# A pooling mixer with its last 32 tokens on quarter-width column tiles, its norm folded into the pooling matrices, and h updated two tiles at a time

## The chip, the cores and the metric

The kernel runs on one core of one Trainium2 chip, in float32 and float32r. The metric is the device time of one launch in microseconds, the median over runs of the same program. Three runs of the kernel before took 953.94, 954.66 and 955.35 us, so its time is 954.66 us.

## The reference, cut to what matters

The program is a decoder trunk of two layers: 16 meta tokens and 256 input tokens (272 together), 1024 channels. Layer 0 mixes tokens with a causal pooling mixer, layer 1 with differential attention; each mixer stands between two SwiGLU feed-forward blocks, and each of these parts sits between two RMS norms. The change touches the pooling mixer of layer 0 alone:

```python
def causal_multiscale_pool(h, w, b, scale):
    ...
    for g, win in enumerate(POOL_WINDOWS):          # 2, 4, 8, 16
        lo = jnp.maximum(t + 1 - win, 0)
        cnt = (t + 1 - lo).astype(jnp.float32)
        pooled.append((csg[:, 1:, g] - csg[:, lo, g]) / cnt[None, :, None])
    pooled = jnp.stack(pooled, axis=2)
    diff = (pooled - hg).astype(h.dtype)
    y = jnp.einsum('blgc,gcd->blgd', diff, w) + b
    return y.reshape(bsz, L, D) * scale
...
    h = h + 0.5 * rmsnorm(f, ffn_norm_post[i, 0])
    hn = rmsnorm(h, mix_norm_pre[i])
    m = causal_multiscale_pool(hn, pool_w[j], pool_b[j], pool_scale[j])
    h = h + rmsnorm(m, mix_norm_post[i])
```

The 1024 channels fall into four groups of 256. Each group has its own window and its own 256x256 matrix `w`. The mean over a window and the subtraction of `hn` are linear in the tokens, so both together are a banded matrix over tokens.

## The kernel before, in words

Activations lie transposed: `h[j]`, j = 0 to 7, is a tile of 128 channels by 272 tokens, and `hall` is all eight side by side. Tokens are stored as the 256 inputs first and the 16 meta tokens last, although the meta tokens come first in time. Every engine works through a list of instructions in the order in which the code issues them (`manual_schedule`), and waits on semaphores that the tile framework puts in; an instruction that waits holds up all that stand behind it on its engine.

The mixer (`pool_mix`, L674 to L776) runs between the first feed-forward block and the second:

- **Residual.** The end of the first block has left its output in `btall`, a first value `old.y` of its post-norm (table lookup, L281) and its sum of squares. VectorE refines the norm by a Newton step (L505, L509) and adds the scaled block output to `h`: first tile 0 by itself (L701, L703, L704), then tile 1 and pairs of tiles (L708 product, L709 sum, sizes in `POOL_H`).
- **Inner product.** For each j, `inner(j)` (L687 to L691) multiplies `h[j]`, as the stationary operand, by `wps[j]`, 256 columns of the group's weights. There are three sets of tokens, `tok` (L680): 0 to 127, 128 to 255, and 144 to 271. The third exists for the 16 meta tokens and the first inputs' neighbours. Results are tokens by channels, in six PSUM banks `z[half][set]`, a half being two groups (512 channels). The two j of a group add up in the same columns.
- **Norm.** ScalarE squares `hall` pair by pair (L711), VectorE adds the squares up (L715 to L718), TensorE sums over the channels for each of the three token sets (L720), and `rsqrt` gives `r2`, one factor per token (L281, L275 to L277). Six of the eight `inner` steps stand ahead of these sums on TensorE and two behind them (`LATE = 2`).
- **Scaled copies.** `normed(q)` (L727 to L734) takes a half of z out of PSUM, multiplied by `r2`, into `zs`: ScalarE and VectorE three copies of 128x512 each.
- **Pooling.** `pooled(j)` (L736 to L751) multiplies `zs` by `bands`, the banded matrices, with three matmuls for each 128 output channels: the tokens 128 to 255, the tokens 0 to 143, and the 32 columns at both ends of y that depend on the meta tokens (L742, L743, L746). Then ScalarE squares the result for the post-norm (L453), and so on into the second feed-forward block, whose first matmuls are L522.

Three things set what waits for what. `warm` (L265) issues matmuls on a constant tile to keep TensorE at work where it would wait: `WARM0 = 12` ahead of the inner products and `WARM2 = 3` behind the pooling. `post.old(j)` (L424 to L431) is a ScalarE product of `h[j]` and a gain that the second feed-forward block needs, for the first three j (`AHEAD[1] = 3`); in the mixer it stands behind the squares (L723). Its output tile `a` is allocated with the tag `xlo{j}` (L426). The pooling weights `wps[q]` were allocated with the tag `xlo{q}` (L664). A tag has one buffer there, so `a` of j lies where `wps[j]` lay.

Line numbers are those of the kernel before. In the changed kernel the lines up to `pool_mix` are four lower: `post.old` is L426 there, the table lookup L277, `inner` L686.

Of the kernel before, what the change touches and what calls it, by code (L numbers as in the profile page):

```python
# [9 lines left out]
F32 = mybir.dt.float32  # L10
# [6 lines left out]
P = 128  # L17
D = 1024
# [34 lines left out]
LATE = 2  # L53

POOL_H = ((0, 1), (1, 2), (2, 4), (4, 6), (6, 8))
POOL_SQ = ((0, 2), (2, 4), (4, 6), (6, 8))
# [5 lines left out]
WARM0 = 12  # L62
# [117 lines left out]
def trunk(ctx, tc, ht, w13a, w13b, w2t, w2n, wqkva, wqkv, wo, wp, lamv, mask, band, gpost, out):  # L180
# [493 lines left out]
    def pool_mix(old, ps, post):  # L674

        def bank():
            return ps.tile([P, 512], F32, tag="bank", name="bank")


        tok = ((0, P), (P, 2 * P), (L - P, L))  # L680

        z = [[bank() for _ in tok] for _ in range(2)]
        sums = bank()[:, 0:3]
# [8 lines left out]

        with tc.tile_pool(name="poolw", bufs=1, reuse_waits="tile") as pw:
            sq = pw.tile([P, NK, L], F32, name="psq")
            zs = [pw.tile([P, D], F32, name=f"zs{ti}", tag=f"zs{ti}") for ti in range(3)]
# [4 lines left out]
            t = tmp.tile([P, L], F32, tag="rt", name="rt")  # L700
            nc.vector.tensor_tensor(t, btall[:, 0], old.y, ALU.mult)  # L701
            old.slope()
            nc.vector.scalar_tensor_tensor(t, old.c, 1.5, t, ALU.add, ALU.mult)  # L703
            nc.vector.tensor_tensor(h[0], h[0], t, ALU.add)  # L704
            old.finish()
            for lo, hi in POOL_H[1:]:
                t = pw.tile([P, 3, L], F32, tag="pt", name="pt", bufs=2)[:, :hi - lo]
                nc.vector.tensor_tensor(t, btall[:, lo:hi], old.r.unsqueeze(1).to_broadcast([P, hi - lo, L]), ALU.mult)  # L708
                nc.vector.tensor_tensor(hall[:, lo:hi], hall[:, lo:hi], t, ALU.add)  # L709
            for lo, hi in POOL_SQ:  # L710
                nc.scalar.activation(out=sq[:, lo:hi], in_=hall[:, lo:hi], func=AF.Square)  # L711
            for j in range(NK - LATE):
                inner(j)
            acc = pw.tile([P, 2, L], F32, name="pacc2")
# [12 lines left out]
            def normed(q):  # L727
                at = slice(q * 512, (q + 1) * 512)
                nc.scalar.mul(out=zs[0][:, at], in_=z[q][0], mul=r2[:, 0:1])
                nc.vector.tensor_scalar(zs[1][:, at], z[q][1], r2[:, 1:2], None, ALU.mult)  # L730
                if q:
                    nc.vector.tensor_scalar(zs[2][:, at], z[q][2], r2[:, 2:3], None, ALU.mult)
                else:
                    nc.scalar.mul(out=zs[2][:, at], in_=z[q][2], mul=r2[:, 2:3])  # L734

            def pooled(j):  # L736
# [5 lines left out]
                nc.tensor.matmul(y[:, P:SEQ], lhsT=zs[1][:, c], rhs=bands[:, g, 0:P], start=True, stop=True)  # L742
                nc.tensor.matmul(y[:, 0:P + NMETA], lhsT=zs[0][:, c], rhs=bands[:, g, 0:P + NMETA],  # L743
                                 start=False, stop=True, skip_group_check=True)
                ends = y.rearrange("p (a b) -> p a b", b=SEQ)[:, :, 0:NMETA]
                nc.tensor.matmul(ends, lhsT=zs[2][:, c],  # L746
                                 rhs=bands[:, g, P + NMETA:].rearrange("p (a b) -> p a b", b=NMETA),
                                 start=False, stop=True, skip_group_check=True)
                post.squared(j, y[:, :L], vt[:, C_PS + j:C_PS + j + 1], pbs[:, j:j + 1], add=False)
# [540 lines left out]
```

## Time and profile before

| what | value |
|---|---|
| median of three runs | 954.66 us (953.94 to 955.35) |
| the profiled execution, its own time | 954.47 us |
| span of that execution, first to last instruction | 952.7 us |
| TensorE matmul rows busy | 940.8 us (99%) |
| weight loads busy | 904.5 us (95%) |
| VectorE, ScalarE, GpSimd busy | 637.2, 501.9, 14.7 us |

The profile is of one execution on the chip. Its times run in microseconds from the span's start. A line of its timeline reads: start, length, engine, source line, operation, output<-inputs, shape, how many instructions were merged into the line, and in brackets how long the engine had stood idle before it and what ended that. PE is TensorE, DVE VectorE, ACT ScalarE, POOL GpSimd. A float32 matmul leaves two records, so 24 records are 12 matmuls. A line of a group reads: source line, engine, operation, names, shape, count, then busy time, mean nanoseconds of one, and idle time before. A line of the windows reads: from:to, length, then busy time and count of PE, PEld (weight loads), DVE, ACT and POOL, then the granted clock of TensorE (1.00 is full speed), the share of DMA and GB/s. The mixer lies between about 206 and 230 us.

### The profile page before, as it was taken

Reading aid. Unit: us, or ns where it says so; the run is one execution under the profiler, and the core shown is the slowest. Engines: PE = TensorE matmul, PEld = TensorE weight load, DVE = VectorE, ACT = ScalarE, POOL = GpSimd, SP = SyncE. Lnnn points to the kernel's source line nnn. Section 1 sums busy time; section 2 is a strip of 40 time slices with the busy share of each in tenths; the row PEclk is TensorE's granted clock in tenths of the full one; section 3 lists DMA queues with packets and bytes.
Section 4 is the critical chain, followed back from the end, with each engine's and each line's share of the span. In section 5 each row is a group of like instructions: output and inputs, shape, how many; then the busy total and the mean of one; then the engine's idle time right before and its main releaser. Section 6 shows DMA issues by size and latency. Waiting matters only on the chain.

```text
span 952.7 us, 17430 instructions
## 1 busy us (share of the span) xinstructions
PE 940.8 (99%) x6937; PEld 904.5 (95%) x6937; DVE 637.2 (67%) x1094; ACT 501.9 (53%) x863; POOL 14.7 (2%) x22
## 2 busy tenths in 40 slices
PE   9999999999999999999999999999999999999997
PEld 9999999998999999999999999999998998888885
DVE  7955554458975555448955554468876899767774
ACT  7744444435654445545744455446776756445442
POOL 0000000210000000000000000000001000000000
PEclk9999999999999999999999999999999999999999
DMA  9755557630375556551755556532523628655521
GB/s 337 239 204 177 166 155 222 219 119 2 116 267 174 175 159 192 179 195 42 257 194 177 163 167 187 187 106 90 177 89 120 212 90 287 223 188 180 185 89 44
DMA packets 48320, 160.74 MB, mean 169 GB/s; under 512 B 5360, under 2 KB 8944, under 8 KB 48240
## 3 DMA queue, kind: packets, MB, share of 16 engines
q1 hardware_dynamic: 47952, 159.31, 52.2%
q8 instruction: 54, 0.88, 0.4%
q10 hardware_dynamic: 288, 0.33, 0.1%
q14 instruction: 26, 0.21, 0.1%
HBM read 158.57 MB, written 1.05 MB: 168 GB/s over the span
## 4 chain that ended last, share of the span: by engine, by line
PE 94%; DVE 3%; ACT 1%; issue 1%; DMA 0%; DVEq 0%; ACTq 0%
PE bank L257 23%; PE bank L256 23%; PE bank L255 23%; PE bank L522 8%; PE bank L1120 7%; PE bank L1122 4%; DVE wlo L149 1%; PE bank L643 1%; PE bank L655 1%; PE bank L644 1%; DMA raw<-in_w13a 0%; ACT sc L844 0%; PE bank L821 0%; PE bank L812 0%; PE bank L811 0%
## 5 line engine op out<-in xcount | busy, mean ns | idle before, releaser
L149 DVE TENSOR_TENSOR wlo<-raw,whi 128x1024 fp32r<-128x1024 f32 (+1 forms) x296 | 353.5, 1197 | 58.9 <-PE bank L256 28.4
L137 ACT CAST whi<-raw 128x1024 fp32r<-128x1024 f32 (+1 forms) x296 | 299.8, 1029 | 51.4 <-PE bank L257 45.9
L255 PE MATMUL bank<-x,whi 128*128 128x272 f32 (+1 forms) x752 | 217.3, 289 | 0.0
L257 PE MATMUL bank<-x,whi 128*128 128x272 f32 (+1 forms) x752 | 216.8, 288 | 0.0
L256 PE MATMUL bank<-x,wlo 128*128 128x272 f32 (+1 forms) x752 | 215.7, 287 | 0.2 <-DVE wlo L149 0.2
L256 PEld LDWEIGHTS bank<-x,wlo 128*128 128x128 f32 x752 | 141.3, 188 | 0.5 <-DVE wlo L149 0.4
L255 PEld LDWEIGHTS bank<-x,whi 128*128 128x128 f32 x752 | 141.3, 188 | 0.5 <-issue 0.4
L257 PEld LDWEIGHTS bank<-x,whi 128*128 128x128 f32 x752 | 141.6, 188 | 0.0
L256 PE MATMUL bank<-ghi,wlo 128*128 128x272 f32 x484 | 140.0, 289 | 0.0
L255 PE MATMUL bank<-ghi,whi 128*128 128x272 f32 x484 | 140.0, 289 | 0.0
L257 PE MATMUL bank<-glo,whi 128*128 128x272 f32 x484 | 140.0, 289 | 0.0
L573 ACT ACTIVATE ua<-ua 128x272 f32<-128x272 f32 (+1 forms) x88 | 37.1, 429 | 143.0 <-DVE ua L559 143.0
L582 ACT CAST ghi<-ua 128x272 fp32r<-128x272 f32 (+1 forms) x88 | 36.1, 417 | 111.7 <-DVE ua L579 111.7
L255 PEld LDWEIGHTS bank<-ghi,whi 128*128 128x128 f32 x484 | 91.8, 190 | 0.0
L257 PEld LDWEIGHTS bank<-glo,whi 128*128 128x128 f32 x484 | 91.2, 188 | 0.0
L256 PEld LDWEIGHTS bank<-ghi,wlo 128*128 128x128 f32 x484 | 90.9, 188 | 0.0
L257 PE MATMUL bank<-xlo,whi 128*128 128x272 f32 x304 | 87.8, 289 | 0.0
L255 PE MATMUL bank<-xhi,whi 128*128 128x272 f32 x304 | 87.4, 287 | 0.0
L256 PE MATMUL bank<-xhi,wlo 128*128 128x272 f32 x304 | 87.3, 287 | 0.0
L579 DVE TENSOR_TENSOR ua<-bank,ua 128x272 f32<-128x272 f32 (+1 forms) x69 | 29.5, 437 | 71.1 <-PE bank L257 71.1
L1120 PE MATMUL bank<-xp,whi 128*128 128x512 f32 x304 | 76.1, 392 | 0.0
L1120 PEld LDWEIGHTS bank<-xp,whi 128*128 128x128 f32 x304 | 55.5, 188 | 10.5
(232 smaller groups left out, 1376.8 us busy)
## 6 DMA issues: line engine op xcount, KB each, us to landing
raw<-in_w13b SPq DMA_DIRECT2D x152, 512.0 KB, 4.1
raw<-in_w2t SPq DMA_DIRECT2D x48, 448.0 KB, 3.4
raw<-in_w2t SPq DMA_DIRECT2D x24, 512.0 KB, 3.5
raw<-in_w2n SPq DMA_DIRECT2D x22, 512.0 KB, 3.8
raw<-in_w13a SPq DMA_DIRECT2D x18, 512.0 KB, 4.2
raw<-in_wqkv SPq DMA_DIRECT2D x18, 512.0 KB, 4.3
raw<-in_wo SPq DMA_DIRECT2D x8, 512.0 KB, 3.7
raw<-in_wqkva SPq DMA_DIRECT2D x6, 512.0 KB, 4.2
```

What stands on the lines that cost most here:

```text
L137: self.nc.scalar.copy(out=hi[:, :n], in_=self.raws[u][:, :n])
L149: self.nc.vector.tensor_tensor(lo[:, :n], raw[:, :n], hi[:, :n].bitcast(F32), ALU.subtract)
L255: nc.tensor.matmul(out_ap, lhsT=a[0], rhs=b[0], start=start, stop=False)
L256: nc.tensor.matmul(out_ap, lhsT=a[1], rhs=b[0], start=False, stop=False)
L257: nc.tensor.matmul(out_ap, lhsT=a[0], rhs=b[1], start=False, stop=stop)
L522: nc.tensor.matmul(us[q][:, :n], lhsT=taken[u][a][:, c * P:(c + 1) * P], rhs=x[:, :n], start=start, stop=stop)
L573: nc.scalar.activation(out=a[:, :self.n], in_=a[:, :self.n], func=AF.Silu)
L579: nc.vector.tensor_tensor(s[:, :n], self.sum(u3), s[:, :n], ALU.mult)
L582: nc.scalar.copy(out=hi, in_=s[:, :n])
L643: nc.tensor.matmul(y[:, :n], lhsT=a[0], rhs=x[0], start=b == 0, stop=False)
L1120: nc.tensor.matmul(u, lhsT=parts[0][:, k * P:(k + 1) * P], rhs=res.pairs[k], start=k == 0, stop=k == NK - 1)
L1122: nc.tensor.matmul(u[:, :n], lhsT=parts[1][:, k * P:(k + 1) * P], rhs=res.x[k][0], start=False, stop=k == NK - 1, skip_group_check=True)
```

## The change

The third token set is replaced by the last 32 tokens alone (240 to 271), since only those are used. Each group's matmul for them (`inner_ends`) has a stationary operand of 32 columns and goes to a quarter of the array's columns and to 32 partitions of one new bank `ze`, one quarter per group, with the j of a group in two rounds (0, 2, 4, 6, then 1, 3, 5, 7). All of it stands behind the sums. The layout of the ends' matrices on the host follows that: the rows of group g hold its matrix, all others are zero.

The norm is no longer multiplied into the copies of z. `zs` takes plain copies, and `r2` is multiplied into the banded matrices instead, giving `sb` (group 0 first, the three others behind), on VectorE, ScalarE and GpSimd. All eight `inner` steps now stand ahead of the sums.

The first two tiles of `h` are updated together, and all pairs follow; the products of the third and fourth pair are issued ahead of their sums. `post.old(0)` and `post.old(1)` are issued ahead of the copies, `post.old(2)` behind the first of the new matrices. The ends of the first output tile come behind the second tile's two main matmuls. `WARM0` is 14.

```diff
-WARM0 = 12
+WARM0 = 14
...
-        tok = ((0, P), (P, 2 * P), (L - P, L))
+        tok = ((0, P), (P, 2 * P))
...
+        ze = bank()
...
+        def inner_ends():
+            for j in (0, 2, 4, 6, 1, 3, 5, 7):
+                g = slice(j // 2 * 32, j // 2 * 32 + 32)
+                nc.tensor.matmul(ze[g, 0:256], lhsT=h[j][:, L - 32:L], rhs=wps[j], start=j % 2 == 0, stop=j % 2 == 1)
...
-            t = tmp.tile([P, L], F32, tag="rt", name="rt")
-            nc.vector.tensor_tensor(t, btall[:, 0], old.y, ALU.mult)
+            t = pw.tile([P, 2, L], F32, tag="pt", name="pt", bufs=3)
+            each = [P, 2, L]
+            nc.vector.tensor_tensor(t, btall[:, 0:2], old.y.unsqueeze(1).to_broadcast(each), ALU.mult)
             old.slope()
-            nc.vector.scalar_tensor_tensor(t, old.c, 1.5, t, ALU.add, ALU.mult)
-            nc.vector.tensor_tensor(h[0], h[0], t, ALU.add)
+            nc.vector.scalar_tensor_tensor(t, old.c.unsqueeze(1).to_broadcast(each), 1.5, t, ALU.add, ALU.mult)
+            nc.vector.tensor_tensor(hall[:, 0:2], hall[:, 0:2], t, ALU.add)
             old.finish()
...
+            product(2)
+            total(2)
+            product(4)
+            product(6)
+            total(4)
+            total(6)
...
-            for j in range(NK - LATE):
+            for j in range(NK):
                 inner(j)
...
+            for j in range(2):
+                post.old(j)
+
+            nc.scalar.copy(out=zs[0][:, 0:512], in_=z[0][0])
+            nc.scalar.copy(out=zs[1][:, 0:512], in_=z[0][1])
             nc.vector.tensor_tensor(acc, sq[:, 0:2], sq[:, 2:4], ALU.add)
...
             for ti, (t0, t1) in enumerate(tok):
                 nc.tensor.matmul(sums[:, ti:ti + 1], lhsT=acc[:, 0, t0:t1], rhs=ones[:, 0:1], start=True, stop=True)
-            for j in range(NK - LATE, NK):
-                inner(j)
-            for j in range(post.ahead):
+            for g in range(4):
+                nc.tensor.matmul(sums[g * 32:g * 32 + 32, 2:3], lhsT=acc[:, 0, L - 32:L], rhs=ones[:, 0:1],
+                                 start=True, stop=True)
+            inner_ends()
+            nc.scalar.copy(out=zs[0][:, 512:1024], in_=z[1][0])
+            nc.vector.tensor_copy(zs[1][:, 512:1024], z[1][1])
+            r2 = rsqrt(sums, 3, True, "rc", 3)
...
+            nc.vector.tensor_scalar(sb[:, 0, 176:], bands[:, 0, 0:P], r2[:, 1:2], None, ALU.mult)
+            nc.scalar.mul(out=sb[:, 0, 0:P + NMETA], in_=bands[:, 0, 0:P + NMETA], mul=r2[:, 0:1])
+            nc.gpsimd.tensor_scalar(sb[:, 0, P + NMETA:176], bands[:, 0, P + NMETA:], r2[:, 2:3], None, ALU.mult)
+            nc.scalar.copy(out=zse, in_=ze[:, 0:256])
+            for j in range(2, post.ahead):
                 post.old(j)
-            r2 = rsqrt(sums, 3, True, "rc", 3)
...
+            nc.vector.tensor_scalar(sb[:, rest, 176:], bands[:, rest, 0:P], r2[:, 1:2], None, ALU.mult)
+            nc.vector.tensor_scalar(sb[:, rest, 0:P + NMETA], bands[:, rest, 0:P + NMETA], r2[:, 0:1], None, ALU.mult)
+            nc.gpsimd.tensor_scalar(sb[:, rest, P + NMETA:176], bands[:, rest, P + NMETA:], r2[:, 2:3], None, ALU.mult)
...
-            normed(0)
-            normed(1)
+            pooled(0)
             for j in range(NK):
-                pooled(j)
+                if j == 0:
+                    pooled(1)
+                elif j > 1:
+                    pooled(j)
+                pooled_ends(j)
```

The order of the instructions on ScalarE, from the squares of `hall` on. A name in brackets is the engine whose semaphore the instruction waits for (its number is the framework's); `a` is the output of `post.old`, `ny` over 128x3 is the table lookup of `r2`. Before:

```order
L711 ACTIVATE psq<-h 128x544 [waits DVE_49] x4
L430 ACTIVATE a<-h 128x272 [waits PE_49,Pool_49] x3
L281 ACTIVATE ny<-bank,eps_c 128x3 [waits PE_49]
L729 ACTIVATE zs_2589<-bank,ny 128x512 [waits DVE_49]
L734 ACTIVATE zs_2591<-bank,ny 128x512
L729 ACTIVATE zs_2589<-bank,ny 128x512 [waits PE_49]
L453 ACTIVATE sq<-bank,pbs,h 128x272 [waits PE_49]
```

The same place on ScalarE after the change:

```order
L725 ACTIVATE psq<-h 128x544 [waits DVE_49] x4
L426 ACTIVATE a<-h 128x272 [waits PE_49,Pool_49] x2
L731 COPY zs_2590<-bank 128x512
L732 COPY zs_2591<-bank 128x512
L743 COPY zs_2590<-bank 128x512
L277 ACTIVATE ny<-bank,eps_c 128x3
L750 ACTIVATE sb<-bands,ny 128x144 [waits DVE_49]
L752 COPY zse<-bank 128x256 [waits PE_49]
L426 ACTIVATE a<-h 128x272 [waits Pool_49]
L449 ACTIVATE sq<-bank,pbs,h 128x272 [waits PE_49]
```

The table lookup now stands behind three copies, and these behind two products `a`; of that row of six instructions only the two `a` wait for TensorE, while the copies and the lookup, which read TensorE's banks, have no wait of their own. The other place is TensorE, from its last inner products ahead of the sums on. Before:

```order
L690 MATMUL bank<-wp,h 128x256 x2
L720 MATMUL bank<-ones,pacc_2635 128x1 [waits DVE_49]
L720 MATMUL bank<-ones,pacc_2635 128x1 x2
L690 MATMUL bank<-wp,h 128x256 [waits DMAHW0_49,Pool_49]
L690 MATMUL bank<-wp,h 128x256 x2
L690 MATMUL bank<-wp,h 128x256 [waits DMAHW3_49,Pool_49]
L690 MATMUL bank<-wp,h 128x256 x2
L742 MATMUL bank<-bands,zs_2590 128x128 [waits DMAHW6_49,DVE_49,PE_49]
L743 MATMUL bank<-bands,zs_2589 128x144 [waits Activation_49]
L746 MATMUL bank<-bands,zs_2591 128x2x16 [waits Activation_49]
```

The same place on TensorE after the change:

```order
L686 MATMUL bank<-wp,h 128x256 [waits DMAHW3_49,Pool_49]
L686 MATMUL bank<-wp,h 128x256
L738 MATMUL bank<-ones,pacc_2601 128x1 [waits DVE_49]
L738 MATMUL bank<-ones,pacc_2601 128x1
L740 MATMUL bank<-ones,pacc_2601 32x1 x4
L692 MATMUL bank<-wp,h 32x256 [waits Activation_49]
L692 MATMUL bank<-wp,h 32x256 x7
L765 MATMUL bank<-sb,zs_2591 128x128 [waits DVE_49,Activation_49]
L766 MATMUL bank<-sb,zs_2590 128x144 [waits Activation_49]
L765 MATMUL bank<-sb,zs_2591 128x128 [waits PE_49]
L766 MATMUL bank<-sb,zs_2590 128x144
L771 MATMUL bank<-sb,zse 128x2x16 [waits Activation_49,Pool_49]
```

Six inner products of full width stood between the sums and the pooling; now eight of 32 columns stand there, and these still read `wps` (the name `wp` in the rows), and the first pooling matmul waits for `sb`, which needs `r2`.

More of the change, by code (lines that the diff above doesn't have):

```diff
@@ L712, in pool_mix, with product, total @@
-            for j in range(NK - LATE):
+            acc = pw.tile([P, 2, L], F32, name="pacc2")
+            more = {}
+            def product(lo):
+                more[lo] = pw.tile([P, 2, L], F32, tag="pt", name="pt", bufs=3)
+                nc.vector.tensor_tensor(more[lo], btall[:, lo:lo + 2], old.r.unsqueeze(1).to_broadcast(each), ALU.mult)
+            def total(lo):
+                nc.vector.tensor_tensor(hall[:, lo:lo + 2], hall[:, lo:lo + 2], more[lo], ALU.add)
+            product(2)
@@ L713, in pool_mix @@
+            total(2)
[3 more added lines that the diff above has]
+            total(6)
+            for lo in (0, 2, 4, 6):
+                nc.scalar.activation(out=sq[:, lo:lo + 2], in_=hall[:, lo:lo + 2], func=AF.Square)
+            for j in range(NK):
                 inner(j)
-            acc = pw.tile([P, 2, L], F32, name="pacc2")
+            for j in range(2):
+                post.old(j)
+            nc.scalar.copy(out=zs[0][:, 0:512], in_=z[0][0])
+            nc.scalar.copy(out=zs[1][:, 0:512], in_=z[0][1])
@@ L741, in pooled, with pooled_ends @@
                 c = slice(j * P, (j + 1) * P)
-                nc.tensor.matmul(y[:, P:SEQ], lhsT=zs[1][:, c], rhs=bands[:, g, 0:P], start=True, stop=True)
-                nc.tensor.matmul(y[:, 0:P + NMETA], lhsT=zs[0][:, c], rhs=bands[:, g, 0:P + NMETA],
+                nc.tensor.matmul(y[:, P:SEQ], lhsT=zs[1][:, c], rhs=sb[:, g, 176:], start=True, stop=True)
+                nc.tensor.matmul(y[:, 0:P + NMETA], lhsT=zs[0][:, c], rhs=sb[:, g, 0:P + NMETA],
                                  start=False, stop=True, skip_group_check=True)
-                ends = y.rearrange("p (a b) -> p a b", b=SEQ)[:, :, 0:NMETA]
-                nc.tensor.matmul(ends, lhsT=zs[2][:, c],
-                                 rhs=bands[:, g, P + NMETA:].rearrange("p (a b) -> p a b", b=NMETA),
+            def pooled_ends(j):
+                ends = ys[j].rearrange("p (a b) -> p a b", b=SEQ)[:, :, 0:NMETA]
+                nc.tensor.matmul(ends, lhsT=zse[:, j % 2 * P:(j % 2 + 1) * P],
+                                 rhs=sb[:, j // 2, P + NMETA:176].rearrange("p (a b) -> p a b", b=NMETA),
                                  start=False, stop=True, skip_group_check=True)
-                post.squared(j, y[:, :L], vt[:, C_PS + j:C_PS + j + 1], pbs[:, j:j + 1], add=False)
+                post.squared(j, ys[j][:, :L], vt[:, C_PS + j:C_PS + j + 1], pbs[:, j:j + 1], add=False)
                 if j:
@@ L1264, in _layout @@
     count = np.minimum(np.concatenate([t[NMETA:], t[:NMETA]]) + 1, win)
+    each = np.where((d >= 0) & (d < win), 1.0 / count, 0.0) - (d == 0)
     ends = np.zeros((P, 4, 2 * NMETA))
-    ends[P - NMETA:] = np.where((d >= 0) & (d < win), 1.0 / count, 0.0) - (d == 0)
+    for g in range(4):
+        ends[g * 32 + NMETA:g * 32 + 32, g] = each[:, g]
     r["band"] = c(np.concatenate([inside, ends], axis=2).astype(np.float32))
```

22 lines of the change are left out of this document (4 added, 18 removed).

## The prediction

> **What bounds the kernel now.** I read the page first. TensorE is busy nearly all the time, and the chain that ended last runs through it:
>
> ```profile
> PE 940.8 (99%) x6937; PEld 904.5 (95%) x6937; DVE 637.2 (67%) x1094; ACT 501.9 (53%) x863; POOL 14.7 (2%) x22
> PE 94%; DVE 3%; ACT 1%; issue 1%; DMA 0%; DVEq 0%; ACTq 0%
> ```
>
> So a microsecond by which the mixer's last matmul moves is a microsecond of the kernel: what follows is TensorE work on weights that are there already. Next I read TensorE's timeline over the mixer:
>
> ```profile
> 206.67 2.84 PE L269 MATMUL bank<-ones 128*128 128x128 f32 x24
> 209.64 8.19 PE L690 MATMUL bank<-wp,h 128*128 128x256 f32 x36
> 217.92 0.83 PE L720 MATMUL bank<-ones,pacc 128*128 128x1 f32 x6
> 218.61 2.84 PE L690 MATMUL bank<-wp,h 128*128 128x256 f32 x12
> 221.29 0.38 PE L742 MATMUL bank<-bands,zs 128*128 128x128 f32 x2
> 226.60 0.30 PE L746 MATMUL bank<-bands,zs 128*128 128x32 f32 x2
> 230.54 1.00 PE L522 MATMUL bank<-x,whi 128*128 128x272 f32 x6 [1.69 <-DVE x L314]
> ```
>
> From 209.64 on, TensorE does not stop until the pooling ends. The pooling begins at 221.29, when the six inner products behind the sums are through; the work on the norm (sums at 217.92, copies from 219.74) lies beneath these. From 221.29 to the next block's first matmul at 230.54 are 9.25 us, and I find nothing in the change that alters them: the count of pooling matmuls and squares is the same. So the question is where the first pooling matmul, at 221.29 now, will stand. The two engines that feed it, VectorE first:
>
> ```profile
> 207.45 0.44 DVE L701 TENSOR_TENSOR rt<-bt,ny 128x272 f32<-128x272 f32 x1 [5.39 <-ACT ny L281]
> 208.14 0.44 DVE L505 SCALAR_TENSOR_TENSOR nt<-bank,nt 128x272 f32<-128x272 f32 x1 [0.25 <-ACT nt L502]
> 208.62 0.44 DVE L703 SCALAR_TENSOR_TENSOR rt<-nt,rt 128x272 f32<-128x272 f32 x1
> 209.10 0.44 DVE L704 TENSOR_TENSOR h<-h,rt 128x272 f32<-128x272 f32 x1
> 209.46 0.43 DVE L509 SCALAR_TENSOR_TENSOR r<-nt,ny 128x272 f32<-128x272 f32 x1
> 209.99 0.44 DVE L708 TENSOR_TENSOR pt<-bt,r 128x272 f32<-128x272 f32 x1
> ...
> 210.83 0.72 DVE L708 TENSOR_TENSOR pt<-bt,r 128x544 f32<-128x544 f32 x1
> 211.58 0.72 DVE L709 TENSOR_TENSOR h<-h,pt 128x544 f32<-128x544 f32 x1
> 212.22 0.72 DVE L708 TENSOR_TENSOR pt<-bt,r 128x544 f32<-128x544 f32 x1
> ...
> 215.01 0.72 DVE L715 TENSOR_TENSOR pacc<-psq 128x544 f32<-128x544 f32 x1
> 215.84 0.73 DVE L716 TENSOR_TENSOR pacc<-pacc,psq 128x544 f32<-128x544 f32 x1
> ...
> 217.43 0.44 DVE L718 TENSOR_TENSOR pacc<-pacc 128x272 f32<-128x272 f32 x1
> ```
>
> and ScalarE:
>
> ```profile
> 215.13 0.66 ACT L711 ACTIVATE psq<-h 128x544 f32<-128x544 f32 x1 [0.74 <-DVE h L709]
> 215.69 1.33 ACT L430 ACTIVATE a<-h 128x272 f32<-128x272 f32 x3
> 218.79 0.26 ACT L281 ACTIVATE ny<-bank,eps_c 128x3 f32<-128x3 f32 x1 [1.76 <-PE bank L720]
> 219.74 0.69 ACT L729 ACTIVATE zs<-bank,ny 128x512 f32<-128x512 f32 x1 [0.69 <-DVE ny L277]
> 220.33 0.68 ACT L734 ACTIVATE zs<-bank,ny 128x512 f32<-128x512 f32 x1
> ```
>
> **Part by part.** *h in pairs.* The Newton step still starts at 208.14. Of two VectorE instructions of 544 columns the second starts 0.75 us later if it needs the first (210.83 to 211.58), else 0.64 later (211.58 to 212.22). The pair's factor comes at 208.62, its sum at 209.37 and ends at 210.09. h[0] was ready at 209.54 and TensorE began 0.10 later; now it begins at 210.19. The 14 warm matmuls instead of 12 reach to about 209.9, so they cost nothing. The factor `r` follows at 210.01, the next product 0.53 later (209.46 to 209.99), so the sums end at 212.01, 213.93 and 214.57.
>
> *Inner products.* Six matmuls took 2.68 us (218.61 to 221.29), 0.447 each. Sixteen stand ahead of the sums, not 18. Four from 210.19, four from 212.11, eight from 214.03 (each time the pair plus 0.10) end at 217.6. The four adds of squares end at 217.35 (three at steps of 0.83 from 214.49, the last 0.44 long), so they are hidden. The two full sums take 0.46 (six records in 0.69 before). The four quarter sums are not in the trace: at least the 0.1 that a change of tiling costs (a step of 0.22 into L811, where the one before is 0.12, in the rows below), at most four more at full price with it, 0.6 to 0.7 in all. I take 0.3, so `inner_ends` begins at 218.4 (218.2 to 218.8).
>
> *`inner_ends`.* Eight matmuls of 256 columns, one after the other 3.6 us; four side by side, 0.9 us. The nearest rows are the attention's matmuls on half the array's rows:
>
> ```profile
> 656.99 0.29 PE L256 MATMUL bank<-x,wlo 128*128 128x272 f32 x1
> 657.11 0.29 PE L257 MATMUL bank<-x,whi 128*128 128x272 f32 x1
> 657.33 0.52 PE L811 MATMUL bank<-kf,qf 64*128 64x144 f32 x4
> 657.68 0.63 PE L812 MATMUL bank<-kf,qf 64*128 64x272 f32 x4
> ...
> 205.46 0.62 PE L470 MATMUL bank<-pacc,ones 128*128 128x272 f32 x2
> ```
>
> Four records of 272 columns on two half tiles take 0.63 us, two records of 272 columns on the whole array 0.62: the halves run side by side. I take 0.9.
>
> *The wait that the change adds.* `a` of j = 0 and 1 lies in the buffer of `wps[0]` and `wps[1]`, which `inner_ends` still reads. So ScalarE, whose two `a` began at 215.7 before, must wait for the first and the fifth matmul of `inner_ends`; three copies and the lookup for `r2` stand behind these, and the matrices `sb` and the first pooling matmul behind the lookup. The fifth matmul is through two rounds of 0.447 and about 0.2 of tail after 218.4, at 219.5. From there: `a` 0.41 to the next (1.33 for three with 0.51 of its own), three copies, lookup to scaled use 0.95 (218.79 to 219.74). The copies and the product `sb` have these nearest rows:
>
> ```profile
> L1140 ACT COPY hn<-bank 128x512 f32<-128x512 f32 x4 | 2.3, 578 | 0.0
> L419 DVE TENSOR_SCALAR b<-bt,h 128x256 f32<-128x256 f32 x4 | 1.4, 353 | 1.1 <-ACT bt L444 1.0
> L666 POOL TENSOR_SCALAR wp<-wp,h 128x256 f32<-128x256 f32 x8 | 9.1, 1150 | 184.1 <-DMA wp<-in_wp 178.5 <-PE bank L257 5.6
> ```
>
> A copy of 0.58 is followed 0.1 before its end (as 219.74 to 220.33 with 0.69), so 0.48 each. A product of 128 columns lies between 0.15 and 0.35; I take 0.26, and 0.10 to TensorE. The sum: 219.5 + 0.41 + 1.44 + 0.95 + 0.36 = 222.66. Against 221.29 the pooling starts **1.4 us later**; with the bounds of the start and of the copies (0.48 to 0.59) 1.1 to 2.0.
>
> *What is hidden.* The other products: VectorE's two of 384 and 432 columns, at the 1.4 ns per column of L419 at most 1.2 us, are first read by the third tile, two tiles of 0.68 (eight take 5.4) after the pooling's start. GpSimd's 32 columns, at 1.15 for 256, have 1.3 us before the first ends. The copy of `ze` and `a` of j = 2 lie on ScalarE beneath the first two tiles. If the cover fails there, 0.2 to 0.4.
>
> *What a pause does to the clock.* `inner_ends` is done at 219.5, so TensorE stands still for 3.2 us. The kernel's one long pause so far is the 1.69 ahead of 230.54. The windows of the granted clock, one over that pause and two behind the last matmul, which is over at 946.10, and TensorE's first rows:
>
> ```profile
> 218.50:231.00 12.50, 10.80 (x77) 9.82 (x77) 9.47 (x22) 9.65 (x19) 0.00 (x0) 1.00 0.00 0
> 946.10:948.70 2.60, 0.00 (x0) 0.00 (x0) 1.83 (x6) 0.98 (x3) 0.00 (x0) 1.00 0.39 135
> 948.80:952.70 3.90, 0.00 (x0) 0.00 (x0) 0.82 (x3) 0.00 (x0) 0.00 (x0) 0.50 0.37 134
> 0.97 3.79 PE L269 MATMUL bank<-ones 128*128 128x128 f32 x16 [0.97 <-POOL ones L233]
> 5.01 1.70 PE L522 MATMUL bank<-xhi,whi 128*128 128x272 f32 x6 [0.25 <-DVE whi L112]
> 6.50 0.99 PE L522 MATMUL bank<-xhi,wlo 128*128 128x272 f32 x6
> ```
>
> A pause of 1.69 leaves the clock at 1.00; 2.6 to 2.7 us after the last matmul it is 0.50. A pause of 3.2 is longer than that. Whether it always does it the trace can't say, since one event has one phase. A slow spell lasted 5.5 us at the program's start (16 records in 3.79, against 24 in 2.84 at 206.67; six take 1.5 from 5.01, the next six with their tail 0.99), so a spell of 0 to 5.5 us at half speed costs 0 to 2.8; I take the middle, 1.4. By the Trainium skill, "TensorE: Matmul & The Clock Gate", Part 1, the clock halves only after an idle window of about 3.4 us, and 3.2 would be too short; this case's trace, with 2.7 us, speaks against so long a threshold.
>
> **The rivals.** The forecast: the wait shifts the pooling by 1.4 and the pause halves the clock for a while, 1.4 more: 954.66 + 2.8 = 957.5. (The profiled execution took 954.47, 0.19 below the median; the sum is a difference, so I add it to the median.)
>
> 1. *The clock holds.* Then 1.4 alone: 956.1. For it: one fall of the clock in the trace, after which nothing came, proves little about a pause that ends. It is also what that rule of the skill would give.
> 2. *The quarter tiles run one after the other.* The fifth matmul is then through three matmuls later, 1.34 us: 954.66 + 2.7 = 957.4. The pause shrinks to 1.8 (eight matmuls end at 222.2, the pooling starts at 224.0), near the 1.69 that left the clock alone. For it: the attention's tiles differ in rows, these in columns. By the Trainium skill, "TensorE: Matmul & The Clock Gate", Part 3, a weight load overlaps a running matmul only if it goes to other rows, and these four share all rows; no row here shows it.
> 3. *Not slower: nothing waits for the weights' buffer.* If the two `a` run at 215.2 as they are written, the copies are done ahead of the sums, the lookup comes at 218.7, and the pooling starts when the matrices are there, 219.65 + 0.36 = 220.0: 1.3 us earlier, 953.4. It decides if ScalarE's `a` begins ahead of 218.4. Against it: the order shows that these two wait for TensorE and that the copies have no wait of their own, which fits only if the `a` wait for something later.
>
> **How the numbers follow.** A measurement of this kernel can tell 0.2%, 1.9 us, from no change. Forecast 0.47, clock holds 0.34, tiles in series 0.12, no wait 0.07. Slower by over 0.2% means above 956.57: the forecast and the series, and 0.03 of the second case, whose shift reaches to 2.0: 0.62. Within 0.2%: 0.31 of the second case and 0.05 of the last: 0.36. Faster, the far end of the last case: 0.02. The range runs from 955.7 (a shift of 1.1 and no slow spell) to 958.7 (2.0 and three quarters of the spell's bound), and leaves out the last case and the far end.
>
> **What would show it.** In the profile after: L426 on ScalarE at 218.9 and 219.5 with TensorE as releaser; the lookup L277 over three columns near 221.4; L692 as eight matmuls in 1.1 us; the first L765 near 222.7 with about 3.2 us of idle time, its end named VectorE or ScalarE; pooling matmuls at twice their spacing and a granted clock under 1.00 for some microseconds behind 222. I am wrong if L426 stands ahead of the sums, if L692 spreads over 3.5 us, or if the pooling starts ahead of 221.3.

## The result and the profile after

| kernel | median | runs | profiled execution | span | first pooling matmul | next block's first matmul |
|---|---|---|---|---|---|---|
| before | 954.31 us | 4, 953.94 to 955.35 | 954.47 us | 952.7 us | 221.29 | 230.54 |
| changed | 960.26 us | 4, 958.97 to 962.1 | 960.17 us | 958.3 us | 222.37 | 236.19 |

The changed kernel is slower: ratio 1.0063, 95% interval 1.0047 to 1.0079. The forecast had the direction and the chain of causes, but 957.5 us and a range up to 958.7: it lost 2.8 us where the chip lost 5.95. Between the two profiled executions lie 5.70 us, and the last two columns hold 5.65 of them: the pooling starts 1.08 us later, and from its first matmul to the next block's first, 9.25 us have become 13.82.

TensorE's timeline over the mixer of the changed kernel (start, length, engine, line, operation, tile on the array, shape, records; in brackets the idle time before the row and what ended it):

```profile
210.10 7.54 PE L686 MATMUL bank<-wp,h 128*128 128x256 f32 x32 [0.25 <-issue]
217.47 0.50 PE L738 MATMUL bank<-ones,pacc 128*128 128x1 f32 x4
217.90 0.24 PE L740 MATMUL bank<-ones,pacc 128*32 128x1 f32 x8
217.99 1.05 PE L692 MATMUL bank<-wp,h 128*32 128x256 f32 x16
222.37 0.77 PE L765 MATMUL bank<-sb,zs 128*128 128x128 f32 x2 [3.33 <-ACT sb L750]
...
229.03 0.77 PE L765 MATMUL bank<-sb,zs 128*128 128x128 f32 x2
229.59 0.69 PE L766 MATMUL bank<-sb,zs 128*128 128x144 f32 x2
230.07 0.47 PE L771 MATMUL bank<-sb,zse 128*128 128x32 f32 x2
230.36 0.77 PE L765 MATMUL bank<-sb,zs 128*128 128x128 f32 x2
...
236.19 1.00 PE L518 MATMUL bank<-x,whi 128*128 128x272 f32 x6 [1.95 <-DVE x L310]
```

Up to 219.04 TensorE keeps to the forecast or is a little ahead of it, the quarter tiles (L692) included: 16 records in 1.05 us. Then it stands for 3.33 us until a matrix `sb` comes from ScalarE. One pooling tile (L765, L766, L771) then takes 1.33 us, 229.03 to 230.36. In the kernels below in which the clock holds, the same tile takes 0.69 (221.30 to 221.99 in the first experiment).

ScalarE's timeline of the changed kernel says where `sb` was kept:

```profile
218.68 0.95 ACT L426 ACTIVATE a<-h 128x272 f32<-128x272 f32 x2 [3.51 <-PE bank L692]
219.54 0.56 ACT L731 COPY zs<-bank 128x512 f32<-128x512 f32 x1
220.01 0.59 ACT L732 COPY zs<-bank 128x512 f32<-128x512 f32 x1
220.48 0.60 ACT L743 COPY zs<-bank 128x512 f32<-128x512 f32 x1
220.96 0.28 ACT L277 ACTIVATE ny<-bank,eps_c 128x3 f32<-128x3 f32 x1
221.94 0.42 ACT L750 ACTIVATE sb<-bands,ny 128x144 f32<-128x144 f32 x1 [0.69 <-DVE ny L273]
```

ScalarE had nothing to do for 3.51 us; its first `a` waited for a quarter tile's matmul, and the copies and the lookup ran behind it back to back. The granted clock (last but two columns: clock, DMA share, GB/s) of one stretch with the pause and three behind it, cut where the trace changes the clock, at 221.483 and 231.723:

```profile
218.07:221.48 3.41, 0.97 (x24) 0.31 (x15) 0.46 (x2) 2.56 (x6) 0.00 (x0) 1.00 0.00 0
221.49:224.89 3.40, 2.52 (x12) 2.55 (x12) 1.42 (x5) 1.16 (x4) 1.12 (x2) 0.50 0.00 0
224.90:228.30 3.40, 3.40 (x17) 3.40 (x17) 1.35 (x3) 2.40 (x5) 0.00 (x0) 0.50 0.00 0
228.31:231.72 3.41, 3.41 (x18) 3.41 (x17) 2.26 (x5) 1.34 (x3) 0.00 (x0) 0.50 0.02 5
```

At half speed for 10.24 us, nearly the whole pooling. All clock changes in the traces of this study are whole multiples of 3.413 us apart, so I speak of windows of 3.413 us. The clock fell at the end of the first one shown, in which TensorE's matmuls were busy for 0.97 us, and it rose after three. The mean granted clock of the four runs was 0.993 to 0.994, so the one profiled was no exception. (One window at half speed takes 0.0018 off the mean over such a span; below I read the number of slow windows of runs without a trace from this, as an estimate.)

The page's totals for the changed kernel, TensorE's row and the chain of work that ended last by engine:

```profile
PE 942.9 (98%) x6947; PEld 906.7 (95%) x6947; DVE 636.8 (66%) x1093; ACT 502.5 (52%) x865; POOL 15.9 (2%) x24
PE 95%; DVE 2%; ACT 1%; issue 1%; DMA 0%; DVEq 0%; ACTq 0%
```

They hide the loss: TensorE is busy 2.1 us longer, although it has less to multiply, since slow matmuls count as busy, and it still makes up the chain. Only the stage's own rows show what happened.

### The profile page after: what moved, and what is told of

It reads as the page before. It is cut to its first block, busy times and chain, and to the rows that moved or that the text cites. A ratio compares the mean times of both kernels' runs of the same rounds, so it can differ in the third digit from the quotient of the medians.

```text
span 958.3 us, 17459 instructions
## 1 busy us (share of the span) xinstructions
PE 942.9 (98%) x6947; PEld 906.7 (95%) x6947; DVE 636.8 (66%) x1093; ACT 502.5 (52%) x865; POOL 15.9 (2%) x24
## 3 DMA queue, kind: packets, MB, share of 16 engines
HBM read 158.57 MB, written 1.05 MB: 167 GB/s over the span
## 4 chain that ended last, share of the span: by engine, by line
PE 95%; DVE 2%; ACT 1%; issue 1%; DMA 0%; DVEq 0%; ACTq 0%
PE bank L253 23%; PE bank L252 23%; PE bank L251 23%; PE bank L518 8%; PE bank L1148 7%; PE bank L1150 4%; PE bank L686 1%; DVE wlo L145 1%; PE bank L639 1%; PE bank L651 1%; PE bank L640 1%; PE bank L765 0%; ACT sc L872 0%; DMA raw<-in_w13a 0%; PE bank L766 0%
```

## The experiments

Theory A, formed from the two profiles: the wait for the weights' buffer makes the pause, the pause halves the clock at the end of a window that is largely idle, and it stays halved until a window is full enough of matmuls. The rivals: the quarter tiles bring the clock down themselves; the chain to `sb` is late without the wait; the length of the pause sets the length of the slow spell. Unless it says otherwise an experiment starts from the changed kernel. The times of the kernel before beside them were 954.1 to 954.35 us.

**The wait removed, by other buffers.** `wps[0]` and `wps[1]` get buffers of their own:

```diff
-    bands = early.enter_context(tc.tile_pool(name="bands", ...)).tile([P, 4, 176], F32, name="bands")
+    own = early.enter_context(tc.tile_pool(name="bands", bufs=1, side="right"))
+    bands = own.tile([P, 4, 176], F32, name="bands")
...
-    wps.append(act.tile([P, 256], F32, tag=f"xlo{q}", name="wp"))
+    wps.append(act.tile([P, 256], F32, tag=f"xlo{q}", name="wp") if q > 1
+               else own.tile([P, 256], F32, tag=f"wp{q}", name="wp"))
```

> The changed kernel, with the pooling weights of j = 0 and 1 in buffers of their own, so that ScalarE's products a of j = 0 and 1 need not wait for the eight matmuls on quarter tiles. Theory (the wait makes TensorE pause, the pause halves its clock): the two a start near 215 instead of 218.7, the first pooling matmul near 220.0 instead of 222.4, the granted clock stays at 1.00 over the pooling; 953.1 us (952.8 to 953.7), 7 below the changed kernel and about 1.2 below the one before. Rival 1 (matmuls on quarter tiles bring the clock down by themselves): the pooling starts as early, but at half speed for some 10 us, 957 to 958. Rival 2 (the chain of copies and products is late without the wait too): the pooling starts near 222, about 960.

Measured: 953.0 us (952.8 to 954.34, 11 runs), ratio 0.9985 (0.9976 to 0.9994). ScalarE's timeline of this kernel (its line numbers are one higher), and then TensorE's:

```profile
214.70 0.92 ACT L427 ACTIVATE a<-h 128x272 f32<-128x272 f32 x2
215.53 0.56 ACT L732 COPY zs<-bank 128x512 f32<-128x512 f32 x1
...
217.84 0.26 ACT L278 ACTIVATE ny<-bank,eps_c 128x3 f32<-128x3 f32 x1 [0.39 <-PE bank L741]
218.80 0.41 ACT L751 ACTIVATE sb<-bands,ny 128x144 f32<-128x144 f32 x1 [0.69 <-DVE ny L274]
...
221.52 3.37 ACT L450 ACTIVATE sq<-bank,pbs,h 128x272 f32<-128x272 f32 x6
```

```profile
219.23 0.46 PE L766 MATMUL bank<-sb,zs 128*128 128x128 f32 x2 [0.56 <-ACT sb L751]
...
226.16 0.72 PE L467 MATMUL bank<-pacc,ones 128*128 128x272 f32 x2 [0.49 <-DVE pacc L461]
226.72 0.62 PE L468 MATMUL bank<-sq,ones 128*128 128x272 f32 x2
228.96 1.00 PE L519 MATMUL bank<-x,whi 128*128 128x272 f32 x6 [1.62 <-DVE x L311]
```

The `a` run at 214.70, the lookup comes right behind the sums, the pause is 0.56 us instead of 3.33, and the clock stays at 1.00 although the quarter tiles are all there. That refutes two rivals: neither do the tiles pull the clock, nor is the chain late by itself. A new wait shows: VectorE's `pacc` holds the post-norm's sums (L467) for 0.49 us, because ScalarE's squares (L450) end later; there are six of them back to back.

**The wait removed, by the order of issue.** The two `a` go behind the copy of `ze`:

```diff
-            for j in range(2):
-                post.old(j)
...
-            for j in range(2, post.ahead):
+            for j in range(post.ahead):
                 post.old(j)
```

> The changed kernel, with the products a of j = 0 and 1 issued behind the copy of ze, where that of j = 2 stands; buffers as in the changed kernel. Theory: the copies and the lookup no longer stand behind a wait; the first pooling matmul near 220.0, clock 1.00; 953.2 us (952.8 to 954.0), at most 0.4 above the kernel with buffers of its own, for 0.8 us more of ScalarE's work now stands between the first matrices and the first square. Rival 1: 957 to 958. Rival 2: about 960.

Measured: 953.23 us (952.64 to 954.3, 11 runs), ratio 0.9984 (0.9976 to 0.9993), the first pooling matmul at 219.26. Two different edits, which only have in common that nothing waits for `inner_ends` ahead of the copies, give the same gain over the changed kernel, 7 us.

**The pause filled, the wait kept.**

```diff
             inner_ends()
+            warm(lambda: idle, ones, 15, P)
```

> The changed kernel with 15 more warm matmuls of 128x128 on the constant tile behind the eight matmuls on quarter tiles, 3.35 us that fill the pause; the wait of ScalarE stays. Theory: the pooling starts at 222.4 as in the changed kernel, but the clock stays at 1.00, so only the later start is left: 955.5 us (955.1 to 956.2). Rival 1 (quarter tiles): the clock falls all the same, about 960. If the lost time were all in the wait and none in the clock: about 960.

Measured: 957.07 us (954.93 to 958.52, 11 runs), ratio 1.002 (1.0011 to 1.0028). The median misses the expected 955.5: four runs took 954.9 to 955.1, seven 956.4 to 958.5. By the span of their instructions alone they form two groups: five of 952.8 to 953.4 us at a mean clock of 0.998 to 0.999, and six of 954.7 to 955.3 at 0.997, one slow window more. The one profiled is of the second group. In its profile the pooling ran at 1.00, as intended, but the clock fell one stage later. TensorE, and the clock of the windows ahead and behind:

```profile
229.12 0.73 PE L466 MATMUL bank<-pacc,ones 128*128 128x272 f32 x2 [0.49 <-DVE pacc L460]
229.68 0.62 PE L467 MATMUL bank<-sq,ones 128*128 128x272 f32 x2
231.92 1.70 PE L518 MATMUL bank<-x,whi 128*128 128x272 f32 x6 [1.62 <-DVE x L310]
```

```profile
219.00:231.56 12.56, 10.81 (x88) 10.11 (x87) 7.72 (x20) 9.98 (x23) 1.12 (x2) 1.00 0.01 1
231.57:234.98 3.41, 3.06 (x13) 3.09 (x14) 3.27 (x9) 0.51 (x2) 0.00 (x0) 0.50 0.00 0
234.99:240.00 5.01, 5.01 (x41) 5.01 (x41) 4.66 (x14) 2.40 (x6) 0.00 (x0) 1.00 0.00 0
```

The two small pauses, 0.49 and 1.62 us, fell into one window, 228.16 to 231.57, and left 0.49 of it idle ahead of L466 and 1.27 behind L467, 1.76 in all. That was enough. The spell lasted one window, over the dense matmuls of the next block. So short pauses add up within a window. The profile also differs far behind the mixer: a wait of 0.83 us ahead of the attention's output projection (731.35 in the kernel before) is not there, so the time flatters this kernel by as much.

**A pause in the kernel before, without quarter tiles.**

```diff
-WARM0 = 12
+WARM0 = 0
```

> The kernel before, without its 12 warm matmuls ahead of the inner products: a pause of 2.8 us there (206.8 to 209.6) with no quarter tile and no wait for a buffer. Theory (a pause alone halves the clock): in those executions where the clock falls, the mixer loses some 4 to 4.5 us, 958 to 959; with 2.8 us, near the 2.7 after which it fell at the program's end, not every execution need show it, the others 954.3. Rival 1 (quarter tiles): 954.3 in all.

Measured: 955.57 us (954.8 to 956.08, 11 runs), ratio 1.0009 (1.0 to 1.0018). TensorE, and the clock from the point where it fell:

```profile
204.70 0.62 PE L470 MATMUL bank<-pacc,ones 128*128 128x272 f32 x2
...
208.88 9.70 PE L690 MATMUL bank<-wp,h 128*128 128x256 f32 x36 [2.81 <-issue]
...
230.93 1.00 PE L522 MATMUL bank<-x,whi 128*128 128x272 f32 x6 [1.68 <-DVE x L314]
...
732.38 0.39 PE L255 MATMUL bank<-ohi,whi 128*128 128x256 f32 x1 [1.50 <-ACT am L871]
```

```profile
209.88:213.29 3.41, 3.41 (x10) 2.65 (x9) 3.34 (x6) 1.62 (x3) 0.00 (x0) 0.50 0.00 0
213.30:230.00 16.70, 15.92 (x101) 14.29 (x99) 11.69 (x25) 10.88 (x22) 0.00 (x0) 1.00 0.01 1
```

A pause of 2.81 us halves the clock where there is no quarter tile at all; this time for one window only. The 36 records of L690 take 9.70 us instead of 8.19. From the sums of the first block's norm (L470, 204.70 here, 205.46 before) to the next block's first matmul (230.93, 230.54 before) it is 26.23 us instead of 25.08: 1.15 us lost, smaller than I expected, since the spell was a single window. Not all of the measured difference is the clock's: the wait ahead of the attention's output projection is 1.50 us here and was 0.83. And two of the eleven runs, 954.8 and 954.93 us, have a mean clock of 0.999 against 0.996 to 0.997 of the other nine: by this, the same pause did not bring the clock down in them.

**The pause's length against the work behind it.** The first experiment's kernel (own buffers) with `WARM0 = 0`, which puts a pause as long as that of the changed kernel ahead of the inner products:

```diff
-WARM0 = 14
+WARM0 = 0
```

> The kernel with buffers of its own, without its 14 warm matmuls: a pause of 3.3 us ahead of the inner products, as long as the changed kernel's, but with dense matmuls of 256 columns behind it. Theory A (a slow spell lasts until the matmuls behind it are dense enough, and the pooling's matmuls are not): a spell of 3.4 us, 1.7 lost, 954.6 us (954.2 to 955.2). Theory B (a longer pause brings a longer spell): a spell of about 10 us, 4 or more lost, 957 to 958.5.

Measured: 954.97 us (953.8 to 955.44, 11 runs), ratio 1.0004 (0.9996 to 1.0013). TensorE and the clock:

```profile
209.82 8.83 PE L687 MATMUL bank<-wp,h 128*128 128x256 f32 x32 [3.38 <-issue]
```

```profile
210.74:214.15 3.41, 3.41 (x9) 2.70 (x8) 3.38 (x7) 1.21 (x2) 0.00 (x0) 0.50 0.00 0
214.16:228.00 13.84, 12.78 (x105) 11.39 (x104) 9.22 (x22) 10.02 (x22) 1.12 (x2) 1.00 0.01 2
```

A pause of 3.38 us, then one window at half speed, not three. In the changed kernel a pause of 3.33 us brought three. The runs form two groups: five took 953.8 to 954.21 us at a mean clock of 0.996, the profiled one among them, and six 954.97 to 955.44 at 0.994 to 0.995. By the mean clock the six had one slow window more; where it lay has no trace, but three windows, as in the changed kernel, would be near 0.993. The length of the pause alone does not set the length of the spell.

**Dense work behind the pause.** The changed kernel, with its wait and its pause, and 14 warm matmuls behind the first ends of the pooling:

```diff
                 pooled_ends(j)
                 if j == 0:
+                    warm(lambda: idle, ones, 14, P)
                     first(0)
```

> The changed kernel with 14 more warm matmuls of 128 columns behind the first ends of the pooling, that is behind the pause and its fall of the clock. They read a constant and nothing waits for their result. They add 1.7 us of work at full speed and 3.3 at half. Theory A (the spell lasts until a window of 3.41 us is filled with dense matmuls): the pooling's own sparse matmuls no longer keep the clock down; the clock is back at 1.00 one window earlier than in the changed kernel or more, after 3.4 or 6.8 us instead of 10.24. Theory B (the pause of 3.3 us sets the length of the spell): 10.24 us again.

Measured: 959.71 us (959.36 to 961.15, 4 runs), ratio 1.0062 (1.0049 to 1.0075). TensorE and the clock:

```profile
221.99 0.46 PE L765 MATMUL bank<-sb,zs 128*128 128x128 f32 x2 [3.34 <-ACT sb L750]
...
223.14 5.00 PE L265 MATMUL bank<-ones 128*128 128x128 f32 x28
```

```profile
223.39:226.80 3.41, 3.41 (x18) 3.41 (x18) 0.56 (x1) 1.00 (x2) 0.00 (x0) 0.50 0.00 0
226.81:236.00 9.19, 7.56 (x60) 6.86 (x59) 5.86 (x14) 6.57 (x13) 0.00 (x0) 1.00 0.01 2
```

The same pause, but the clock is back after 3.41 us instead of 10.24. TensorE takes 5.00 us for work that nobody needs, and from the first pooling matmul to the next block's, at 236.07, it is 14.08 us, only 0.26 more than in the changed kernel. (The kernel's time is not a fair comparison, for the wait of 0.84 us ahead of the attention's output projection, which the changed kernel has, is gone here.) The mean clock of the four runs was 0.995 to 0.997, against 0.993 to 0.994. This is the test that decides between the theories, as far as it goes: by the busy time, the second slow window of the changed kernel was as full as this one, with the pooling's matmuls, and the clock stayed down behind it; here, behind warm matmuls, it rose. Two things differ besides the work: the pause ended 1.40 us ahead of the edge here, while in the changed kernel its last 0.89 us lay in the first slow window; and the third slow window there, also of pooling matmuls, did bring the clock back.

**A shorter pause.** Two warm matmuls in the pause instead of 15:

```diff
             inner_ends()
+            warm(lambda: idle, ones, 2, P)
```

> The changed kernel with two warm matmuls behind the ends' products. ScalarE's wait for the weights' buffers stays, so the pooling starts where it did, near 222.3; TensorE's pause ahead of it shrinks from 3.34 us to some 2.9. Theory A (the pause halves the clock if it fills enough of one 3.41 us window, and the spell lasts until the matmuls behind it fill a window again): the pause is still long enough in some phases of the grid; where the clock falls the spell is three windows again, 10.2 us, and the kernel takes 959 to 960; where it holds, 955.5. Two groups of times, then, with nothing between. Theory B (the length of the spell follows the length of the pause): a shorter spell, 5 to 7 us, and 956.5 to 957.5 in all runs.

Measured: 957.8 us (955.99, 956.96, 956.99, 958.62, 960.48, 961.9), ratio 1.0052 (1.0037 to 1.0067). Neither expectation was met as written. The runs do not form two groups, and they are not all between 956.5 and 957.5 either: with the pause 0.63 us shorter two of six take as long as the changed kernel, and one is free. Their mean clocks, 0.999 for the fastest down to 0.993 and 0.994 for the slowest, fit spells of none to three windows, but only the fastest has a trace. In that one the clock held:

```profile
222.28 0.46 PE L766 MATMUL bank<-sb,zs 128*128 128x128 f32 x2 [2.70 <-ACT sb L751]
...
232.02 1.00 PE L518 MATMUL bank<-x,whi 128*128 128x272 f32 x6 [1.62 <-DVE x L310]
```

This run is the best control for the changed kernel: the same wait and the same order of the pooling at full clock. From the first pooling matmul to the next block it takes 9.74 us, against 9.25 before and 13.82 after. So of the lost 4.57 us, 0.49 belong to the order of the pooling and 4.08 to the clock.

**The squares in time.** The first experiment's kernel, with each tile's ends directly behind its main matmuls:

```diff
-            pooled(0)
             for j in range(NK):
-                if j == 0:
-                    pooled(1)
-                elif j > 1:
-                    pooled(j)
+                pooled(j)
                 pooled_ends(j)
```

> The kernel with buffers of its own for the weights of j = 0 and 1, and the ends of the first output tile issued right behind its two main matmuls, no longer behind the second tile's. Theory (the order of the ends delays the first square by 0.5 us and ScalarE's chain of squares never makes it up): first square 0.8 us behind the first pooling matmul instead of 1.35, no 0.5 us of idle time ahead of the post-norm's sum, 952.5 us (952.3 to 952.9), 0.5 below the kernel with buffers of its own. Rival (the ends' matrices or the copy of ze are not there in time): TensorE waits as long ahead of the first ends, 953.0.

Measured: 952.67 us (952.24 to 952.97, 11 runs), ratio 0.9983 (0.9974 to 0.9992). The pause of 0.49 us ahead of the post-norm's sums is gone, from the first pooling matmul to the next block's it is 9.33 us (219.03 to 228.36) instead of 9.73, and the median is 0.33 us lower.

**Warm matmuls ahead of the next block.** The last kernel, and:

```diff
             post.rms(lambda: s, True)
+            warm(bank, ones, 7, P)
```

> The kernel of early_ends, with 7 warm matmuls of 128x128 behind the post-norm's sum, which fill the pause of 1.6 us ahead of the second feed-forward block. Theory (a pause of 1.6 us halves the clock in some executions): the lowest times stay at 952.3 to 952.6, the times 1.3 us or more above the lowest go away, median 952.4. Rival (the pause does nothing to the clock): the same spread and median as early_ends; or 0.1 to 0.3 more if the last warm matmul runs into the block's first one.

Measured: 951.92 us (951.65 to 952.24, 9 runs), ratio 0.9974 (0.9964 to 0.9984). This beats both kernels: 2.3 us below the one before. But why? TensorE's pause ahead of the next block is filled, and five hundred microseconds later the wait of 0.84 us ahead of the attention's output projection is gone too. So the gain of 0.75 us over the last kernel could come from either. The same seven matmuls in the kernel with the filled pause:

> The kernel of fill_pause, whose executions took from 954.9 to 958.5 us, with 7 more warm matmuls behind the post-norm's sum. Theory (what was left there is the clock falling in the two later pauses of 0.5 and 1.6 us): 954.9 to 955.3 in nearly all executions, median 955.1. Rival (the spread has another source): median 957 and a spread of 3 us as before.

Measured: 958.53 us (956.82 to 959.19, 5 runs), ratio 1.0041 (1.0029 to 1.0054). Missed by over 3 us, although the clock in the profile stayed at 1.00 throughout the mixer. The place is again that projection:

```profile
733.64 0.38 PE L251 MATMUL bank<-ohi,whi 128*128 128x256 f32 x1 [2.18 <-DVE of L931]
```

Its first matmul waits 2.18 us there, for a VectorE result. The kernel with the filled pause alone had no wait there, and the kernel before one of 0.83, so the seven matmuls, which gained by this place in the last kernel, lost 2.18 us by it here. My reading is that the added tile in PSUM changes which banks the later tiles get, and with them who must be done before the first of them can be written; the traces show the waits and what ended them, not the banks. The other four runs, up to 959.19, have no trace, and what they lost beyond that stays open.

**Bank or clock?** Two kernels were to tell this apart. The first takes only the bank, without a matmul (`warm(bank, ones, 0, P)`):

> The fastest kernel so far without its seven warm matmuls ahead of the second feed-forward block, but with the PSUM bank that they were written to still taken out of the rotation. Theory C (that kernel's gain of 0.75 us over the one before it came from the bank: every later result lies one bank further, and the wait of 0.84 us ahead of the attention's output projection is gone): 951.9 again, no idle time ahead of that projection, the pause of 1.68 us ahead of the second block still there. Theory D (the gain came from the warm matmuls, which keep the clock up in runs that the profile does not show): 952.67, with the same gap ahead of the projection or none.

Measured: 952.6 us (952.28 to 953.0, 11 runs), ratio 0.9983 (0.9974 to 0.9992), the wait of 0.84 us still there. It decides nothing, since the wait that it was to move stood where it was: it seems that a bank to which nothing is written is not taken. The second has six matmuls instead of seven, with which the wait at the projection stays:

```diff
-            warm(bank, ones, 7, P)
+            warm(bank, ones, 6, P)
```

> The fastest kernel so far with six warm matmuls instead of seven ahead of the second feed-forward block. With six, the program's first matmul of the attention's output projection still waits for a ScalarE copy of the last attention head (the operand am) before it may write its PSUM bank; with seven it lies in a bank that came free earlier. Theory C (seven gained 0.75 us because that wait of 0.84 us is gone): 952.6, the gap of 0.84 us near 728 is there. Theory D (the gain came from the warm matmuls, which shorten the pause ahead of the second block and keep the clock up): six do nearly what seven do, 952.0 with the gap.

Measured: 952.62 us (952.32 to 953.18, 11 runs), ratio 0.998 (0.9971 to 0.9989). TensorE of this kernel, ahead of the next block and of the projection:

```profile
228.96 0.99 PE L519 MATMUL bank<-x,whi 128*128 128x272 f32 x6 [0.35 <-DVE x L311]
...
729.75 0.39 PE L252 MATMUL bank<-ohi,whi 128*128 128x256 f32 x1 [0.84 <-ACT am L897]
```

Six matmuls fill the pause down to 0.35 us and gain nothing (952.67 without them); with the seventh the wait of 0.84 us goes, and 0.7 are gained. The mixer itself decides it: from the first pooling matmul to the next block's it is 9.33 us with none, with six (219.63 to 228.96) and with seven (219.13 to 228.46). So the fastest kernel owes 0.7 us to a wait far behind the mixer that went by luck, and only the rest, down to 952.6, to the mixer.

## Why the prediction was wrong

The step that failed is the size of the slow spell: "so a spell of 0 to 5.5 us at half speed costs 0 to 2.8; I take the middle, 1.4". It lasted 10.24 us and cost 4.08, beyond the bound I had called an end. The 5.5 us came from the program's start, where dense warm matmuls and the first block's run; I carried this length over to a place where the pooling's matmuls of 128, 144 and 32 columns run. The traces with dense work behind the pause show that the pause alone does not set the length: one window with inner products or warm matmuls, three with the pooling. The other steps, in the prediction's order:

- *h in pairs, 16 inner products, sums.* TensorE began at 210.10 (210.19 forecast), and the first sum stands at 217.47 (217.6). The quarter sums took 0.09 us, not 0.3: `inner_ends` began at 217.99, not 218.4.
- *Side by side.* Right: 1.05 us (0.9). The weight loads and the matmuls of the changed kernel's quarter tiles (count, least, median and longest duration in ns, first and last start):

```profile
L692 PEld LDWEIGHTS bank<-wp,h x16: 110/112/114, 218.0 to 218.4; 128*32 128x32 f32 x16
L692 PE MATMUL bank<-wp,h x16: 378/379/383, 218.0 to 218.7; 128*32 128x256 f32 x16
```

  Sixteen records of 0.379 us each begin within 0.7 us, so they overlap, and the rival in which they run in series is refuted. The four tiles differ in columns and share all rows. By the Trainium skill, "TensorE: Matmul & The Clock Gate", Part 3, a weight load overlaps a running matmul only if it goes to other rows; this trace disagrees: four loads begin at 218.21 to 218.23, while the four matmuls begun at 217.99 to 218.01 ran until 218.37 to 218.39.
- *The wait.* Right in its place, its cause and what stands behind it; the pooling started 1.08 us later (1.4; `inner_ends` began 0.41 earlier than forecast, which is more than the difference). The rival in which nothing waits is refuted by the row of L426, and two kernels without the wait show that all the rest hangs on it.
- *"9.25 us ... I find nothing in the change that alters them".* Wrong by 0.49 us. The work is the same, but the first ends stand behind the second tile, so the first square starts later and ScalarE runs late up to the post-norm's sums. Moving the ends back removed that pause and 0.40 us.
- *What is hidden.* Right. VectorE's three products took 0.29, 0.48 and 0.50 us and GpSimd's two 0.48 and 0.67, and no pooling tile in the profile after waits for them:

```profile
221.94 0.29 DVE L749 TENSOR_SCALAR sb<-bands,ny 128x128 f32<-128x128 f32 x1
222.14 0.48 DVE L755 TENSOR_SCALAR sb<-bands,ny 128x384 f32<-128x384 f32 x1
222.53 0.50 DVE L756 TENSOR_SCALAR sb<-bands,ny 128x432 f32<-128x432 f32 x1
```

- *The clock falls.* Right, against the rival in which it holds. The pause was 3.33 us (3.2), of which 2.45 lay in the window that brought the fall. By the Trainium skill, "TensorE: Matmul & The Clock Gate", Part 1, the clock halves only after an idle window of about 3.4 us, and the windows run freely at 3413 ns; the second agrees with the traces, the first does not: TensorE was busy for 0.97 us of that window.

With the measured sizes the sum is 1.08 + 0.49 + 4.08 = 5.65, against 5.70 between the two profiled executions.

What stays open: by the profile's busy time the second slow window of the changed kernel is as full (3.40 of 3.40 us) as the third, after which the clock rose, and as the one slow window of the experiment with dense work. Which measure of activity the clock goes by is not visible in these columns. A count of the columns that the rows stream comes closer. At half speed a pooling tile streams 608 (two records each of 128, 144 and 32) in 1.33 us, which is about 1,560 in a window; the warm matmuls and the inner products reach 2,050 to 2,130, and the first slow window of the changed kernel, with the rest of the pause in it, about 1,180. At full speed (a quarter tile counted as a quarter) the clock fell behind mixer windows of 880 to 1,530, and it held behind 1,525 and 1,630 in the kernel with the shorter pause. So by this count the pooling at half speed lies close to the edge, but the second and third slow windows differ by less than the rows cut at their ends. This is an estimate from the rows, which no run tested.

## What to carry to other kernels

Before an edit puts a reader of a buffer late, look for who takes that buffer next and what is queued behind that one on its engine; here two products that nobody needed yet held up the copies and the norm's lookup. Price a pause of TensorE not by its own length alone but by where it falls in the windows and by what runs behind it: here the pooling's short matmuls stayed at half speed for three windows, dense ones left it after one. And before a gain of less than a microsecond is put down to an edit, look through the whole trace for waits that have moved elsewhere.

## What the runs showed of the hardware

- In the mixer the clock fell at the end of windows of 3.413 us in which TensorE stood idle for 1.76 us (0.49 and 1.27, the kernel with the filled pause) to 2.49 us (207.33 to 209.82, own buffers without warm matmuls). It held over a pause of 2.70 us that lay across two windows, with 1.75 us of it in the first (219.58 to 221.33). The two ends are so close that idle time alone may not be the measure.
- By the mean clock some runs of the kernel before had a window at half speed too: of the 33 runs beside the first four experiments 22 took 953.73 to 954.55 us at 0.998 to 0.999, and eleven 955.16 to 955.77 at 0.996 to 0.997, which fits one slow window. Its pause of 1.69 us may bring it in some phases; no such run has a trace.
- A change of TensorE's tiling from 128 to 32 columns cost less than 0.1 us (217.90 to 217.99 for the four quarter sums), and GpSimd's product of 32 columns took 0.48 us, of 96 columns 0.67.
